# A hybrid encoder layer on one core: value and gate projections moved among output blocks, first tokens transposed on TensorE, x prepared in first slots

## The chip, the cores and the metric

The kernel runs on one core of a Trainium2 chip. The metric is the device time of one execution in microseconds (us). The engines are named as in the profile: PE (TensorE, matrix products), DVE (VectorE), ACT (ScalarE), POOL (GpSimd), and SP, which here only issues DMAs. Each engine runs its own instructions strictly in the order in which the program was written for it.

## The reference

One layer over two sequences (1024 and 4096 tokens, model width 1024), with the same weights:

```python
proj = rms_norm(x, norm_g) @ w_in      # q 512 | k 128 | v 128 | gate 512 | GLU 2 x 512 | gate 512
attn = windowed_gqa(q, k, v, sink)     # 8 heads of 64, 2 kv heads, |t-s| <= 128, 128-query blocks
conv = conformer_conv(u_conv, ...)     # value * sigmoid(gate) -> depthwise conv of 31 taps
                                       # -> LayerNorm -> swish
mix  = concat([attn * silu(g_attn), conv * silu(g_conv)])
y    = rms_norm(x + mix @ w_out, final_g)
```

## The kernel before

The tokens are cut into ten groups of 512 (two from the first sequence, eight from the second), each of four blocks of 128. To keep float32 accuracy with float16 products, every operand is split into a high and a low float16 part, and a product is three matmuls. `inproj` (L413 to L420) thus issues 24 matmuls of 512 columns for one tile of 128 output channels: 8 slices of the model width times 3.

There are two stages. **Stage A** (attention) works with ten weight tiles per group (k, v, four q, four gates). The walk over groups is a walk over "slots", one for each query block: `slot` emits the attention of the block, then work that prepares the groups ahead: `prep_x` for group gi+2 (load a block of x, sum of squares on ACT, reciprocal root on POOL, split on ACT and DVE, transposing DMA), and a share of the projections of group gi+1. At the end of a group `split_late` prepares two weight tiles of stage B. After groups 6 and 7 `max_wout` loads w_out in order to find its largest entry, and `scale_wout` turns that into a power of two; for this it sends one row through PE and back (L396, L402), with two PSUM buffers of the tag `s`, which has three and which the attention scores (L564, L565) use too. Attention results are parked in DRAM.

**Stage B** (convolution and output) has twelve weight tiles per group: eight of value and gate, `glu` (two tiles and two evictions for each of four channel blocks j; L717 on ACT, L718 on DVE, into the tile `h`), and four of the convolution's gate, `conv_gate`. `start_b` loads the 2 MB of transposed x of a group. `conv_chunk` runs the 31 taps of the convolution as DVE instructions (L800 to L804), one for each tap and channel block, in the two pairs j = 0, 1 and j = 2, 3. In all groups but the first the last four taps are made by ACT products (L784, L786) that accumulating DMAs issued by POOL add into `pa`, and the first tap instruction of a pair on DVE (L800) reads `pa`. `ln_batch` transposes the result on PE (L815) and makes the LayerNorm statistics on DVE; `ln_act` transposes back (L854). `out_first` and `out_second` make the output projection of a block (48 matmuls at L873, 24 from the attention half `ma` and 24 from the convolution half `mc`), add x by an accumulating DMA, and normalize (a reciprocal root of seven small steps on POOL, L293 to L301, then L925 on DVE).

The order is not the order of emission. The class `Plan` collects all steps with a cost, their reads and writes, and `flush` lists them anew: whichever step can start first by the costs goes next, and on a tie the one that was emitted first. Two rules of it matter below. Buffers of one tag are handed out in the order in which their first use was emitted. And the resulting order of each engine is fixed; what is late on the chip is waited for in place.

The beginning: `load_first` loads four blocks of x (L237), `prep_first` (L463 to L480) makes squares, one reciprocal root for all four blocks, the split and four transposing DMAs; `first_weights` loads, multiplies by norm_g (L315), scales and splits the weight tiles (L322 to L356).

Of the kernel before, what the change touches and what calls it, by code (L numbers as in the profile page):

```python
# [9 lines left out]
F16 = mybir.dt.float16  # L10
# [7 lines left out]
P = 128  # L18
# [190 lines left out]
def hymba_kernel(ctx, tc, x_p, x_s, w_in, norm_g, sink, dw_w, vecs, w_out, final_g, dist, y_p, y_s):  # L209
# [97 lines left out]
    def load_w(c, early):  # L307
# [5 lines left out]
        dma(lambda: w.t, lambda: w_in[c], 524288, [x16[0]] if 6 <= c < NT_A else [], [w])  # L313
# [146 lines left out]

    def prep_first(x16, xbs):
        ms, v, rs = (small(smx, NB, t, 1) for t in ("ms4", "v4", "rs4"))
        xts = []  # L463
        for b, xb in enumerate(xbs):
            xt = pl.buf(pxA, [P, 2, D], F16, "xt", 2) if b < 2 else pl.buf(pat, [P, 2, D], F16, "pT", 3)
            pl.op("ACT", c_act(1024) + 100, lambda b=b, xb=xb, xt=xt: S.activation(xt.t[:, 1], xb.t, AF.Square, scale=1.0 / math.sqrt(D), accum_out=ms.t[:, b : b + 1]), [xb], [(xt, 1), (ms, b)])
            xts.append(xt)
        pl.op("DVE", 85, lambda: V.tensor_scalar(v.t, ms.t, EPS, XSCALE ** -2, ALU.add, ALU.mult), [ms], [v])
        y = small(smx, NB, "y4", 2, I32)
        pl.op("DVE", 85, lambda y=y: V.tensor_scalar(y.t, v.t.bitcast(I32), -0.5, 1597463007.0, ALU.mult, ALU.add), [v], [y])  # L470
        yv = lambda y=y: y.t.bitcast(F32)
        for it in range(3):
            a, z = small(smx, NB, "a4", 2), rs if it == 2 else small(smx, NB, "z4", 2)
            pl.op("DVE", 105, lambda a=a, yv=yv: V.tensor_tensor(a.t, yv(), yv(), ALU.mult), [y], [a])
            pl.op("DVE", 105, lambda a=a: V.scalar_tensor_tensor(a.t, a.t, -0.5, v.t, ALU.mult, ALU.mult), [a, v], [a])
            pl.op("DVE", 105, lambda a=a, z=z, yv=yv: V.scalar_tensor_tensor(z.t, a.t, 1.5, yv(), ALU.add, ALU.mult), [a, y], [z])
            y, yv = z, (lambda z=z: z.t)
        for b in range(NB):
            split_x(x16, b, xbs[b], xts[b], rs, lambda b=b: rs.t[:, b : b + 1])
        store_x(0, x16)  # L480

# [529 lines left out]
```

## Time and profile before

| | us |
|---|---|
| median of 3 runs (lowest to highest) | 1930.12 (1929.18 to 1932.13) |
| the profiled execution | 1927.47 |
| its span, first to last instruction | 1925.7 |

The profiled execution is 2.65 us under the median, and 1.77 us of it lie around the span. The page gives busy time for each engine, a strip of 40 slices, a chain of work that ended last, and groups of instructions. A busy PE in it is not a PE at its peak. Every view used here names the source line, the engine and the tiles, written `out<-in`; a bracket at the end of a row says how long the engine stood idle before the instruction and what ended the wait. PEclk is the share of the full TensorE clock that was granted.

### The profile page before, as it was taken

The page shows a single profiled execution, that of the slowest core. Times are in us where ns is not written, and L with a number is a line of the kernel's source. Part 1 is how long each engine was busy: PE and PEld are TensorE (multiplying, and loading weights), DVE is VectorE, ACT ScalarE, POOL GpSimd, SP SyncE. Part 2 cuts the span into 40 slices and gives each one's busy share as a digit, 9 for nine tenths or more (in the row PEclk, how much of TensorE's full clock was granted, in tenths as well). Part 3 has the DMA queues.
Part 4 walks back from the last instruction along what each step waited for, and adds up shares of the span by engine and source line. Part 5 has one row for each costly group of instructions (what it writes and reads, how often), then busy time and mean ns, then how long its engine had stood idle before and what let it go on. Part 6 is the DMA issues. An engine that isn't in the chain of part 4 may idle for free.

```text
span 1925.7 us, 25978 instructions
## 1 busy us (share of the span) xinstructions
PE 1816.8 (94%) x8956; PEld 852.0 (44%) x8956; DVE 1666.9 (87%) x3550; ACT 1027.2 (53%) x2181; POOL 606.3 (31%) x830
## 2 busy tenths in 40 slices
PE   3999999999999998989999999999999999999957
PEld 1444444444444443434444444444444444444433
DVE  6688996989999959879989999896969879696997
ACT  3587786887887838754324343433424243434323
POOL 1422233232321200000171725254361717152444
PEclk9999999999999998999999999999999999999979
DMA  8477987999889997664424444443443343443314
GB/s 256 124 156 195 199 198 192 181 234 224 179 211 242 196 267 159 137 169 118 103 69 95 94 88 106 87 110 88 105 103 99 99 105 93 92 117 77 76 56 115
DMA packets 373765, 270.15 MB, mean 140 GB/s; under 512 B 329344, under 2 KB 331008, under 8 KB 371072
## 3 DMA queue, kind: packets, MB, share of 16 engines
q1 hardware_dynamic: 359616, 221.03, 44.6%
q0 software_dynamic: 14016, 47.45, 14.0%
q8 instruction: 70, 1.15, 0.2%
q14 instruction: 63, 0.52, 0.1%
HBM read 100.41 MB, written 58.72 MB: 83 GB/s over the span
## 4 chain that ended last, share of the span: by engine, by line
PE 60%; DVE 24%; ACT 7%; POOL 5%; issue 3%; DMA 1%; SPq 0%; DVEq 0%; ACTq 0%; POOLq 0%
PE mm L420 39%; PE mm L873 15%; DVE acc L804 7%; DVE pe L568 4%; DVE pe L588 3%; ACT pe L576 2%; PE o L603 2%; ACT pe L587 2%; POOL rn_a L300 1%; DVE qst L530 1%; PE s L564 1%; POOL v L916 1%; PE s L565 1%; PE c L854 1%; DVE xt L448 1%
## 5 line engine op out<-in xcount | busy, mean ns | idle before, releaser
L420 PE MATMUL mm<-x,wA 128*128 128x512 f16 x4800 | 1083.3, 381 | 16.8 <-DMA x<-xd 8.8
L420 PEld LDWEIGHTS <-wA 128*128 128x128 f16 x4800 | 468.6, 98 | 562.0 <-issue 23.1
L804 DVE SCALAR_TENSOR_TENSOR acc<-h,taps,acc 128x512 f32<-128x512 f32 (+2 forms) x1244 | 710.1, 640 | 0.0
L873 PE MATMUL mm<-wo,mc 128*128 128x512 f16 x960 | 217.2, 383 | 3.7 <-ACT mc L864 3.5
L873 PE MATMUL mm<-wo,ma 128*128 128x512 f16 x960 | 213.7, 379 | 0.0
L568 DVE CUSTOM_DVE_ANT_0 pe<-s,dist_sb,sink_sb 128x384 f32<-128x384 f32 (+1 forms) x320 | 199.9, 659 | 11.3 <-PE s L565 9.1
L588 DVE SCALAR_TENSOR_TENSOR pe<-pe,rc 128x384 f16<-128x384 f32 (+1 forms) x320 | 189.0, 630 | 15.9 <-ACT pe L587 15.0
L587 ACT ACTIVATE pe<-pe,rc 128x384 f16<-128x384 f32 (+1 forms) x320 | 175.6, 594 | 36.3 <-DVE rc L582 21.3
L576 ACT ACTIVATE pe<-pe,nm 128x384 f32<-128x384 f32 (+1 forms) x320 | 188.5, 590 | 2.4 <-DVE nm L568 2.1
L240 POOL DMA_DIRECT2D pa<-pp x54 | 49.0, 908 | 316.2 <-ACT pp L786 195.7
L873 PEld LDWEIGHTS <-mc 128*128 128x128 f16 x960 | 94.5, 99 | 113.8 <-ACT mc L864 4.1
L873 PEld LDWEIGHTS <-ma 128*128 128x128 f16 x960 | 93.8, 98 | 112.5
L717 ACT ACTIVATE h<-mm,ucolh 128x512 f32<-128x512 f32 x40 | 27.5, 687 | 181.2 <-PE mm L420 181.2
L861 ACT ACTIVATE xn<-c,vec_sb 128x128 f32<-128x128 f32 x160 | 60.2, 457 | 109.7 <-PE c L854 109.7
L564 PE MATMUL s<-kst,qst 128*128 128x384 f16 (+1 forms) x320 | 102.3, 321 | 14.1 <-DVE nm L568 12.0
L420 PE MATMUL mm<-x,xt 128*128 128x512 f16 x480 | 105.6, 379 | 0.0
L300 POOL TENSOR_SCALAR rn_a<-rn_y,v 128x1 f32<-128x1 f32 x76 | 101.6, 1337 | 7.6
L565 PE MATMUL s<-kst,qst 128*128 128x384 f16 (+1 forms) x320 | 101.9, 320 | 0.0
L914 ACT ACTIVATE sq<-yb 128x512 bf16<-128x512 f32 x80 | 49.3, 618 | 97.5 <-DMA yb<-x_s 64.0
L916 POOL TENSOR_SCALAR v<-ms 128x1 f32<-128x1 f32 x38 | 66.1, 1739 | 92.9 <-ACT sq L914 91.1
L440 POOL TENSOR_SCALAR msv<-ms 128x1 f32<-128x1 f32 x36 | 8.5, 236 | 266.6 <-ACT xt L439 266.2
L603 PE MATMUL o<-pT,vst 128*64 128x512 f16 x696 | 84.4, 388 | 0.0
(181 smaller groups left out, 1969.7 us busy)
## 6 DMA issues: line engine op xcount, KB each, us to landing
pa<-pp POOLq DMA_DIRECT2D x48, 512.0 KB, 4.5
xd<-x SPq DMA_DIRECT2D x10, 2048.0 KB, 7.4
x<-xd SPq DMA_DIRECT2D x10, 2048.0 KB, 7.9
xb<-x_s SPq DMA_DIRECT2D x32, 512.0 KB, 4.7
yb<-x_s POOLq DMA_DIRECT2D x30, 512.0 KB, 5.5
y_s<-yb SPq DMA_DIRECT2D x30, 512.0 KB, 2.6
md<-mx SPq DMA_DIRECT2D x40, 256.0 KB, 2.6
ma<-md SPq DMA_DIRECT2D x40, 256.0 KB, 3.1
```

The lines of the kernel that those rows point to most:

```text
L300: pl.op(eng, cost, lambda: en.tensor_scalar(a.t, view(cur), view(cur), v.t, ALU.mult, ALU.mult), [cur, v], [a])
L420: T.matmul(ps.t, w16.t[:, a, k, :], x16.t[:, b, k, :], start=(k == 0 and i == 0), stop=(k == KD - 1 and i == 2))
L564: T.matmul(sv(), q, kst.t[:, 2 * kv, kc0 : kc0 + n], start=True, stop=False)
L565: T.matmul(sv(), q, kst.t[:, 2 * kv + 1, kc0 : kc0 + n], start=False, stop=True)
L568: pl.op("DVE", 198 + n / 0.96, lambda: V.tensor_tensor_reduce(sc_(hh), sv(), dist_b.t[:, kv, d0 : d0 + n], gcol[:, hh : hh + 1], sink_sb[: ...
L576: pl.op("ACT", 280 + 0.834 * n, lambda hh=hh: S.activation(sc_(hh), sc_(hh), AF.Exp, bias=nm.t[:, hh : hh + 1], scale=-1.0, accum_out=den. ...
L587: pl.op("ACT", c_act(n, 1), lambda hh=hh: S.activation(p16(hh, 0), sc_(hh), AF.Copy, scale=rc.t[:, hh : hh + 1]), [rc, (pe, hh + 2)], [(pe ...
L588: pl.op("DVE", c_dve(n, 1), lambda hh=hh: V.scalar_tensor_tensor(p16(hh, 1), sc_(hh), rc.t[:, hh : hh + 1], p16(hh, 0), ALU.mult, ALU.subt ...
L603: T.matmul(o.t[r], vst.t[:, vb % NB, lo, kv, :], mov, start=(i == 0 and m == 0), stop=(i == nk - 1 and m == 2))
L804: pl.op("DVE", c_dve(n, 1), lambda: V.scalar_tensor_tensor(a.t[:, :n], src(), w, a.t[:, :n], ALU.mult, ALU.add), hr + [a], [a])
L873: T.matmul(po[hf].t, m.t[:, a, k - k0, :], wo.t[:, k, b, hf * 512 : (hf + 1) * 512], start=(k == 0 and a == 0 and b == 0), stop=(k == KD - ...
L916: pl.op(eng, 900 if en is GP else 140, lambda: en.tensor_scalar(v.t, ms.t[:, 0:1], ms.t[:, 1:2], EPS, ALU.add, ALU.add), [ms], [v])
```

## The change

Seven edits, all in what is emitted and when:

1. The four first blocks of x are no longer split on ACT and DVE and transposed by DMA. Blocks are scaled in place (DVE for two, ACT for two), PE transposes them in float32 (8 steps of 4 transposes), ACT evicts the high part and DVE the low part. The reciprocal root is made twice, for two blocks each.
2. The first loads come in the order norm_g, x block 0, weight k, x blocks 1 to 3.
3. Group 0 is projected in the order k, v, two gates, four q, two gates, and the weights are made ready in that order.
4. The multiplication by norm_g moves for tiles 3, 5, 6 and 7 to ACT, in eight instructions of 128 columns each.
5. All four `prep_x` of a group are emitted in its first slot.
6. `split_late` is emitted after slots 1 and 2 instead of after the last slot.
7. In stage B `start_b` and `glu` of group gi+2 are emitted among the output blocks of group gi (the load with the first block, the four channel blocks after the second and third), and no longer at the head of group gi+1.

```diff
-        dma(lambda: w.t, lambda: w_in[c], 524288, [x16[0]] if 6 <= c < NT_A else [], [w])
+        dma(lambda: w.t, lambda: w_in[c], 524288, [x16[0]] if 8 <= c < NT_A else [], [w])
+        if c in (3, 5, 6, 7):
+            def by_k():
+                for k in range(KD):
+                    S.activation(w.t[:, k], w.t[:, k], AF.Copy, scale=ng.t[:, k : k + 1])
+            pl.op("ACT", 2340, by_k, [ng, w], [w])
+            return w
...
+    def first_block(x16, b, xb, rs, c):
+        if b % 2 == 0:
+            pl.op("DVE", c_dve2(1024, 1), lambda: V.tensor_scalar(xb.t, xb.t, rs.t[:, c : c + 1], None, ALU.mult), [xb, rs], [xb])
+        else:
+            pl.op("ACT", c_act(1024, 1), lambda: S.activation(xb.t, xb.t, AF.Copy, scale=rs.t[:, c : c + 1]), [xb, rs], [xb])
+        for hf in range(2):
...
+                def tr():
+                    for k in range(4):
+                        T.transpose(pv()[:, k, :], xb.t[:, (4 * hf + k) * P : (4 * hf + k + 1) * P], ident)
+                pl.op("PE", 900, tr, [xb], [pt])
+                pl.op("ACT", c_act(512), lambda: S.activation(dst(0), pv(), AF.Copy), [pt], [(x16, (b, hf, 0))])
+                pl.op("DVE", c_dve(512), lambda: V.tensor_tensor(dst(1), pv(), dst(0), ALU.subtract), [pt, (x16, (b, hf, 0))], [(x16, (b, hf, 1))])
...
-    for t in range(NT_A):
+    for i, t in enumerate((T_K, T_V, 6, 7, 2, 3, 4, 5, 8, 9)):
...
-            for b in range(i * NB // nb, (i + 1) * NB // nb):
+            for b in range(NB if i == 0 else 0):
                 prep_x(gi + 2, x16[gi + 2], b)
...
-        if gi < 6:
-            for c in (2 * gi, 2 * gi + 1):
+            if gi < 6 and i in (1, 2):
+                c = 2 * gi + i - 1
                 wd[c] = split_late(NT_A + c)
...
+    curs[1] = start_b(1, curs[0])
+    load_out(curs[1]["x"])
+    for j in range(4):
+        glu(curs[1], j)
     for gi in range(NG):
         si, g, n_g = groups[gi]
-        if gi + 1 < NG:
-            curs[gi + 1] = start_b(gi + 1, curs[gi])
...
-            for j in range(4):
-                glu(curs[gi + 1], j)
...
                 out_second(gi, b0 + i, po, mc[i], fast(b0 + i, 2))
+                if gi + 2 < NG and nb > 1:
+                    if i == 0:
+                        curs[gi + 2] = start_b(gi + 2, curs[gi + 1])
+                    else:
+                        for j in range(4)[-4 + 2 * (i - 1) :][: 2 if i < nb - 1 else 4]:
+                            if j not in curs[gi + 2].setdefault("glu", []):
+                                curs[gi + 2]["glu"].append(j)
+                                glu(curs[gi + 2], j)
```

What the lists of instructions show of it, at three places. First PE at the very beginning, before the change (`x_0` is the transposed x of group 0, `wA_40` the weight tile k, `w_mx` and `w_mr` largest entries of weights on their way to a power of two):

```order
L330 MATMUL s_213<-ident,w_mx_208 1x128
L341 MATMUL s_226<-w_e_37_218,ones 128x2
L330 MATMUL s_233<-ident,w_mx_224 1x128
L341 MATMUL s_250<-w_e_46_242,ones 128x2
L330 MATMUL s_287<-ident,w_mr_282 1x128
L341 MATMUL s_300<-w_e_70_290,ones 128x2
L420 LDWEIGHTS wA_40_238
L420 MATMUL mm_306<-x_0_259,wA_40_238 128x512
```

and with it:

```order
L337 MATMUL s_201<-ident,w_mx_197 1x128
L348 MATMUL s_230<-w_e_44_224,ones 128x2
L509 MATMUL mm_248<-ident,xb_167 128x128 x4
L509 MATMUL mm_253<-ident,xb_167 128x128 x4
...
L509 MATMUL mm_304<-ident,kst_175 128x128 x4
L509 MATMUL mm_311<-ident,kst_175 128x128 x4
L337 MATMUL s_323<-ident,w_mx_316 1x128
L427 LDWEIGHTS wA_47_286
L427 MATMUL mm_343<-x_0_258,wA_47_286 128x512
```

PE now makes the transposes of x itself (eight rows of four, two of them left out here), and the row that belongs to the scale of the four q tiles (`w_mr`) is no longer ahead of the first projection matmul.

Second, PE in the last stretch of stage A, where the row of `scale_wout` passes (`w_mr` again). Before, with the projections of group 8 around it (`wA_77` and `wA_79` are the third and fourth q tile) and the first scores of group 8 behind it (`kst_6844` is its k):

```order
L420 MATMUL mm_7892<-x_3368_7271,wA_77_339 128x512
L396 MATMUL s_7924<-ident,w_mr_7922 1x128
L420 LDWEIGHTS wA_79_350
L420 MATMUL mm_7926<-x_3368_7271,wA_79_350 128x512
...
L420 MATMUL mm_7926<-x_3368_7271,wA_79_350 128x512
L402 MATMUL s_7944<-w_e_3805_7938,ones 128x2
L564 LDWEIGHTS qst_6294
L564 MATMUL s_7946<-kst_6844,qst_6294 128x384
```

and with the change, where `wA_56` is the tile v of group 8 and `kst_6926` its k:

```order
L427 MATMUL mm_7850<-x_3375_7163,wA_56_389 128x512
L403 MATMUL s_7858<-ident,w_mr_7844 1x128
L427 LDWEIGHTS wA_56_389
L427 MATMUL mm_7850<-x_3375_7163,wA_56_389 128x512
...
L409 MATMUL s_7909<-w_e_3812_7871,ones 128x2
L598 LDWEIGHTS qst_6421
L598 MATMUL s_7911<-kst_6926,qst_6421 128x384
L599 LDWEIGHTS qst_6421
L599 MATMUL s_7911<-kst_6926,qst_6421 128x384
```

The row goes through PE in the second projection tile of group 8, no longer in the sixth, and the scores of group 8 follow there. Before, no score stands on PE between the last ones of group 7 and this row, which is 153 projection matmuls; with the change the longest such stretch anywhere in stage A is 96.

Third, DVE where the last group (9) begins in stage B. Before (`h_8325` is the tile h of group 9, the rows L819 are the statistics of group 8, `pa_16824` the ACT products of group 9, `acc_8778` its sum):

```order
L718 SCALAR_TENSOR_TENSOR h_8325_15998<-h_8325_15998,mm_16787 128x512
L925 SCALAR_TENSOR_TENSOR yb_16715<-yb_16715,r_8309_16885,fg 128x1024
L718 SCALAR_TENSOR_TENSOR h_8325_15998<-h_8325_15998,mm_16881 128x512
L819 BN_STATS bst_17013<-c_17002 128x6
L718 SCALAR_TENSOR_TENSOR h_8325_15998<-h_8325_15998,mm_16941 128x512
...
L837 SCALAR_TENSOR_TENSOR nmr_17065<-mv_17030,lrs_17064 128x4
L800 SCALAR_TENSOR_TENSOR acc_8778_17089<-h_8325_15998,taps,pa_16824 128x512
L800 SCALAR_TENSOR_TENSOR acc_8778_17096<-h_8325_15998,taps,pa_16824 128x512
L804 SCALAR_TENSOR_TENSOR acc_8778_17089<-h_8325_15998,taps,acc_8778_17089 128x512
```

and with it, under the new line numbers (L755 evicts a value tile into h, L837 is the first tap of a pair, L841 a tap, L856 the statistics; `h_8194`, `acc_8785` and `pa_16731` are those of group 9):

```order
L902 TENSOR_TENSOR mc_16860<-xn_16842,mc_16860 128x512
L755 SCALAR_TENSOR_TENSOR h_8194_15949<-h_8194_15949,mm_16873 128x512
L837 SCALAR_TENSOR_TENSOR acc_8785_16974<-h_8194_15949,taps,pa_16731 128x512
L837 SCALAR_TENSOR_TENSOR acc_8785_16984<-h_8194_15949,taps,pa_16731 128x512
L841 SCALAR_TENSOR_TENSOR acc_8785_16974<-h_8194_15949,taps,acc_8785_16974 128x512
...
L962 SCALAR_TENSOR_TENSOR yb_16878<-yb_16878,r_8315_17023,fg 128x1024
L755 SCALAR_TENSOR_TENSOR h_8194_15949<-h_8194_15949,mm_16932 128x512
L841 SCALAR_TENSOR_TENSOR acc_8785_16974<-h_8194_15949,taps,acc_8785_16974 128x512
...
L856 BN_STATS bst_17119<-c_17094 128x6
```

With the change the first tap of group 9 stands behind the eviction of its third channel block, and 23 tap instructions of group 9 stand ahead of the statistics of group 8; before, none does. The eviction of the fourth channel block (the second L755 row) stands behind the tap that reads `pa`.

## Rows read from the trace of the kernel before

**Rows 1.** Windows: length; busy PE, PEld, DVE, ACT, POOL; PEclk; DMA share; GB/s.

```profile
104.00:860.00 756.00, 726.38 (x3806) 337.61 (x3804) 654.33 (x1656) 585.89 (x1357) 157.23 (x355) 0.99 0.86 195
1100.00:1765.00 665.00, 665.00 (x3173) 312.92 (x3172) 566.86 (x925) 247.18 (x467) 274.46 (x259) 1.00 0.41 98
1765.00:1926.00 161.00, 128.41 (x604) 62.34 (x602) 145.67 (x336) 55.86 (x119) 63.85 (x66) 0.91 0.33 81
```

**Rows 2.** Timeline, opening: start, length, engine, line, operation.

```profile
4.08 1.06 ACT L466 ACTIVATE xt<-xb 128x1024 f16<-128x1024 f32 x1 [2.05 <-DMA xb<-x_p]
9.29 1.06 ACT L466 ACTIVATE pT<-kst 128x1024 f16<-128x1024 f32 x1
10.96 1.22 DVE L315 TENSOR_TENSOR pe<-pe,ng 128x1024 f32<-128x1024 f32 x1
26.32 5.31 SPq L243 DMA_TRANSPOSE x<-pT  x2
34.17 0.35 SPq L237 DMA_DIRECT2D xd<-x  x1
36.45 17.84 PE L420 MATMUL mm<-x,wA 128*128 128x512 f16 x69
```

**Rows 3.** Timeline, other stretches: prices of the operations that are added.

```profile
57.22 0.66 PE L517 MATMUL s<-ident,vt 128*128 128x128 f32 x4
58.76 0.67 DVE L522 TENSOR_TENSOR vst<-s,vst 128x512 f16<-128x512 f32 x1
...
731.07 2.12 ACT L587 ACTIVATE pe<-pe,rc 128x384 f16<-128x384 f32 x4
...
1770.37 0.16 DVE L829 TENSOR_SCALAR lv<-mv 128x4 f32<-128x4 f32 x1
...
1772.54 0.16 DVE L837 SCALAR_TENSOR_TENSOR nmr<-mv,lrs 128x4 f32<-128x4 f32 x1
```

**Rows 4.** Waits of PE from 104 to 860: total us, times, longest.

```profile
PE s L564 <- DVE nm L568: 11.8, 19, 1.5
PE mm L420 <- DVE qst L530: 6.8, 1, 6.8
PE s L341 <- DVE w_e L337: 3.5, 3, 2.0
```

**Rows 5.** Timeline of DVE and ACT, 700 to 720.

```profile
704.46 1.22 DVE L389 TENSOR_REDUCE wmx<-xb 128x1 f32<-128x1024 f32 x1 [7.60 <-DMA xb<-w_out]
...
718.23 0.63 ACT L610 ACTIVATE mx<-t 128x512 f16<-128x512 f32 x1 [20.90 <-DVE t L609]
```

**Rows 6.** Timeline of PE, then of DVE, 1750 to the end.

```profile
1724.19 41.60 PE L420 MATMUL mm<-x,wA 128*128 128x512 f16 x192
1765.63 1.91 PE L815 MATMUL c<-ident,acc 128*128 128x128 f32 x16
...
1853.92 0.48 PE L815 MATMUL c<-ident,wA 128*128 128x128 f32 x1 [11.90 <-DVE wA L804]
...
1756.19 0.69 DVE L718 SCALAR_TENSOR_TENSOR h<-h,mm 128x512 f32<-128x512 f32 x1 [7.71 <-ACT h L717]
1766.27 0.70 DVE L819 BATCH_NORM_STATS2 bst<-c 128x6 f32<-128x512 f32 x1 [9.39 <-PE c L815]
...
1772.62 1.41 DVE L800 SCALAR_TENSOR_TENSOR acc<-h,taps,pa 128x512 f32<-128x512 f32 x2
...
1779.79 16.64 DVE L804 SCALAR_TENSOR_TENSOR acc<-h,taps,acc 128x512 f32<-128x512 f32 x25
...
1902.03 0.70 DVE L819 BATCH_NORM_STATS2 bst<-c 128x6 f32<-128x512 f32 x1 [1.60 <-PE c L815]
```

**Rows 7.** Timeline of DVE and POOL around 958, then POOL around 1760.

```profile
955.89 15.98 DVE L804 SCALAR_TENSOR_TENSOR acc<-h,taps,acc 128x512 f32<-128x512 f32 x24
...
958.94 13.11 POOL L916 TENSOR_SCALAR v<-ms 128x1 f32<-128x1 f32 x1 [0.24 <-ACT sq L914]
...
1759.55 0.86 POOL L240 DMA_DIRECT2D pa<-pp  x1 [4.20 <-DMA pa<-pp]
```

More of the change, by code (lines that the diff above doesn't have):

```diff
@@ L459, in load_first @@
         return xb
-    def prep_first(x16, xbs):
[L462 to L479, printed above, removed]
-        store_x(0, x16)
@@ new lines, in square_first, with chain @@
+    def square_first(xbs):
+        ms = [small(smx, 2, "ms4", 2) for _ in range(NB // 2)]
+        for b, xb in enumerate(xbs):
+            sq = pl.buf(pxA, [P, 2, D], F16, "xt", 2)
+            m = ms[b // 2]
+            pl.op("ACT", c_act(1024) + 190, lambda b=b, xb=xb, sq=sq, m=m: S.activation(sq.t[:, 1], xb.t, AF.Square, scale=1.0 / math.sqrt(D), accum_out=m.t[:, b % 2 : b % 2 + 1]), [xb], [sq, (m, b % 2)])
+        return ms
+    def prep_first(x16, xbs):
+        for i, ms in enumerate(square_first(xbs)):
+            v, a, rs = (small(smx, 2, t, 2) for t in ("v4", "a4", "rs4"))
+            y = small(smx, 2, "y4", 2, I32)
+            def chain(ms=ms, v=v, a=a, rs=rs, y=y):
+                V.tensor_scalar(v.t, ms.t, EPS, XSCALE ** -2, ALU.add, ALU.mult)
+                V.tensor_scalar(y.t, v.t.bitcast(I32), -0.5, 1597463007.0, ALU.mult, ALU.add)
+                z = y.t.bitcast(F32)
+                for it in range(3):
+                    V.tensor_tensor(a.t, z, z, ALU.mult)
+                    V.scalar_tensor_tensor(a.t, a.t, -0.5, v.t, ALU.mult, ALU.mult)
+                    V.scalar_tensor_tensor(rs.t, a.t, 1.5, z, ALU.add, ALU.mult)
+                    z = rs.t
+            pl.op("DVE", 1900, chain, [ms], [v, a, rs, y])
+            for b in (2 * i, 2 * i + 1):
+                first_block(x16, b, xbs[b], rs, b % 2)
+        store_x(0, x16)
@@ L616, in hymba_kernel @@
     smA = pool(st_a, "smA", side="right")
-    wA, wd = [], {}
+    wA, wd = {}, {}
     x16 = {0: new_x16(0)}
     own = {0: new_group(0)}
-    xbs = [load_first(b) for b in range(NB)]
     dma(lambda: ng.t, lambda: norm_g, 4096, [], [ng])
+    xbs = [load_first(0)]
     w_k = load_w(T_K, True)
+    xbs += [load_first(b) for b in range(1, NB)]
     prep_first(x16[0], xbs)
@@ L637, in hymba_kernel @@
     dma(lambda: taps, lambda: dw_w, 63488, [], [taps_b])
+    first_weights([T_G])
+    first_weights([T_G + 1])
     first_weights([2, 3, 4, 5])
@@ L647, in hymba_kernel @@
     x16[1] = new_x16(1)
-    for t in range(NT_A):
+    for i, t in enumerate((T_K, T_V, 6, 7, 2, 3, 4, 5, 8, 9)):
         group_proj(0, x16[0], own[0], None, t)
-        if t < 4:
-            first_weights([T_G + t])
-        elif t < 4 + NB:
-            prep_x(1, x16[1], t - 4, [x16[0]])
+        if t in (6, 7):
+            first_weights([t + 2])
+        elif 4 <= i < 4 + NB:
+            prep_x(1, x16[1], i - 4, [x16[0]])
     def slot(gi, blocks, i, qb):
@@ L676, in hymba_kernel @@
             slot(gi, blocks, i, qb)
-        if gi < 6:
-            for c in (2 * gi, 2 * gi + 1):
+            if gi < 6 and i in (1, 2):
+                c = 2 * gi + i - 1
                 wd[c] = split_late(NT_A + c)
-        else:
+        if gi >= 6:
             if gi == 6:
```

11 lines of the change are left out of this document (6 added, 5 removed).

## The prediction

> **What bounds the kernel now.** I read the stages first, each as one window [rows 1]. From 1100 to 1765 us PE is busy for 665.00 us of 665.00 at full granted clock, DVE for 567: there PE alone sets the time, and nothing that moves work on other engines can shorten it. Before that, from 104 to 860 us (stage A), PE is busy for 726 of 756 us, with DVE at 654 and the DMA engines at 0.86: PE paces it too, but it loses 30 us in waits. After it, from 1765 to the end, PE is busy for 128 of 161 us and DVE for 146: the end belongs to DVE. And ahead of all, the first projection matmul runs at 36.45 us [rows 2]. So there are three places to win: the opening, the waits in stage A, the end. The timeline shows what each hangs on. In the opening the fourth block of x is squared at 9.29, the last pair of transposing DMAs goes at 26.32 and takes SP 5.31 us, the store of the finished x, which needs the last of them, goes at 34.17, and PE starts 2.3 us later [rows 2]. In stage A the largest waits of PE are for scores (11.8 us in 19 pieces), one of 6.8 us, and 3.5 us for the scale of a weight [rows 4]. The 6.8 us have a history: ACT stood idle for 20.90 us up to 718 and DVE for 7.60 us up to 704, where it waits for a block of w_out [rows 5]. `scale_wout` holds two of the three `s` buffers in the queue of that tag, so that no score of group 8 can be placed ahead of it, and PE runs projections only; then the scores come in a heap, and PE waits for the softmax. At the end, finally, PE does the LayerNorm transposes of group 8 at 1765.63; DVE, which had idled 7.71 and 9.39 us just before, starts the taps of group 9 at 1772.62 and is busy to the end; PE has nothing left at 1842.0 and waits 11.90 us for these taps [rows 6].
>
> **The opening.** Removed: the split on DVE (four instructions of about 1.2 us) and four transposing DMAs. Added, with prices from [rows 3]: 8 x 4 transposes on PE at 0.66 us for four (5.3 us, at a time when PE has nothing else), 8 evictions on ACT and 8 on DVE (0.67), a second root of 11 steps (twelve take 2.33 us, so 2.1), and 32 ACT instructions of 128 columns. For the last, ACT takes 1.06 us for 1024 columns [rows 2] and 0.53 for 384 (a quarter of 2.12 [rows 3]), which makes 0.32 for 128 and 0.64 for 512. The path, by the new order of each engine: weight k now lands between x blocks 0 and 1. Five loads came within 6.9 us after the first (4.08 to 10.96 [rows 2]), some 1.7 us each, so that the second block lands at 8.5 and the fourth at 11. First root: square of block 1 at 9.8, eleven steps, 12.1. Second root behind four scalar steps (0.8) and one scaling (0.8): 15.7. From there ACT has in a row: scaling of block 3 (1.06), three evictions (1.9), the split of k (1.06), one eviction (0.64), eight small instructions (2.5), three evictions (1.9): 24.8, and DVE's last subtraction 25.5. First projection matmul at 25.5 in place of 36.45, **11 us** sooner. Two of them are lost again: v can't start before its weight has gone through DVE (0.8 of scalar steps, two maxima of about 1.2, another 1.2 of scalar steps, one product of 1.2, one split of 1.3 after 25.5, so 32.4; PE is done with k at 31.7), and the scales of later tiles stand within the k and v matmuls. **-9 us**. Bounds: -4 if the small ACT instructions cost what 384 columns cost (0.2 us more each, with up to 24 of them ahead of the v tile), -12 if nothing is lost.
>
> **Stage A.** The number of matmuls, scores and softmax steps stays. With all `prep_x` in the first slot, the blocks of w_out that `max_wout` loads get their buffers sooner, and the row of `scale_wout` passes PE four projection tiles earlier, with scores around it. The heap goes, and with it the 6.8 us [rows 4]. The two PE steps of a late weight's scale now always have matmuls between them, so most of the 3.5 us goes as well. The 11.8 us for scores I leave. **-9 us**. Bounds: what is late next is the softmax, since the first slot now carries four preparations on ACT and DVE beside attention; if the waits for scores grew by half I would lose 6, with the rest unchanged a net of +3. If half of the 30 us of PE's waits went, -15. I take the value near the row that has a cause.
>
> **Stage B up to 1765.** The load of x for group gi+2 is issued a whole iteration sooner, and two channel blocks are projected between output blocks. PE was full and stays full: 0. Between 860 and 1100 the same DVE work and the same first load open the stage: 0, bounds -4 and +4.
>
> **The end.** 23 taps of group 9 now stand ahead of the statistics of group 8. One costs 16.64/25 = 0.67 us [rows 6], so 15.3 us of the DVE work that PE waited for moves into the 7.71 + 9.39 = 17.1 us in which DVE idled. The last LayerNorm transposes but for those of the single closing block come at 1853.92 - 15.3 = 1838.6. PE must not be later than that: it was through at 1842.0, but 22 matmuls of an output block, 0.217 us each (192 take 41.60 [rows 6]), now follow the transposes in place of preceding them, 4.8 us, so 1837.2. From there DVE has the same 48 us up to the closing statistics at 1902.03 [rows 6] as before, and the tail behind it stays. **-15 us**; bounds -8 (if `pa` or the normalization on POOL holds DVE back half as long as it idled) and -18.
>
> **Sum.** -9 - 9 - 15 = -33 on the profiled execution of 1927.47, which is 1894.5. The median of the runs shown lies 2.65 above that execution, so I forecast **1897 us**.
>
> **Rivals.** *The opening's gain dies in stage A.* If stage A were paced by DMA or softmax and not by PE, an earlier start would only lengthen the waits; speaking for it are DMA shares of 0.86 and DVE at 87%, against it 96% on PE [rows 1]. Only the end is left: 1930 - 15 = 1915. *The end doesn't move*, because DVE waits in place for `pa` where it idled before: 1930 - 18 = 1912. For it speaks that POOL adds three times in series, the last add issued at 1759.55 [rows 7], some 6 us ahead of the transposes of group 8; against it, that the second channel block now ends four tiles and two output blocks ahead of these transposes (192 matmuls at 0.217 us, 42 us), and before four tiles (21 us). *The order hardly changes the chip's time*, as each piece was hidden already: 1930.
>
> *Slower.* The eviction of the fourth channel block stands on DVE behind the tap that reads `pa`. If `pa` is late, that PSUM buffer stays full and PE stops, in each of the eight groups from 2 to 9. The price is lateness beyond a point: two tiles and an output block (96 matmuls, 21 us) lie between the third block and the transposes, the buffer is needed 7 us behind these (the transposes, 1.9 us, and one tile, 5.2 us), 7 us of DVE work stand between, so `pa` may come 21 us after the third block. I expect it 3 us before that block: some 18 us after the second one, as before (tiles done at 1724.19 + 20.8 [rows 6], last add issued at 1759.55 [rows 7], and its transfer). Lateness of 24 us costs nothing; to lose the 33 us won and 7 on top takes 5 us per group more, so 29 us, and gives 1937. The trace shows a cause that could do it: a POOL step on one value per partition took 13.11 us at 958.94, and ended just when the row of 24 taps on DVE ended (955.89 + 15.98 = 971.87) [rows 7]. Two to three such steps in every group ahead of the adds would be enough. The Trainium skill (GPSIMD Engine Reference, section 1, Specifications) says that POOL shares its SBUF interfaces with VectorE and contends with DVE instructions that have two SBUF inputs. By that rule the taps that now fill DVE's pauses slow POOL's steps more often than before; this trace agrees with it at 958.94, by the 13.11 us beside the 16 us of taps. It makes me leave the end's bound at -8. Against the rival: POOL was busy for 274 us of 665 in stage B [rows 1], stretched steps included.
>
> **How the numbers follow.** Forecast with its terms in their bounds (1882 to 1910): 0.64. Opening lost in stage A: 0.14. End not moved: 0.13. No change: 0.03. Slower: 0.06. About 0.2% (4 us) is what a measurement of this kernel tells from no change. Faster 0.64 + 0.14 + 0.13 = 0.91, same 0.03, slower 0.06. The range takes the forecast's own 1882 and reaches up to the two rivals at 1912 and 1915, so 1882 to 1916; outside are the rivals of no gain, and the tails of the bounds.
>
> **What would show it.** First projection matmul at 24 to 28 us. In stage A no wait of PE for a score's PSUM or for q above 3 us near the end, and its idle time under 24 us. From 1100 on PE at 100% as before. DVE without a pause in the 20 us ahead of the transposes of group 8, and the wait of PE ahead of those of group 9 (11.90 us) down to under 3. The prediction is wrong if stage A ends less than 10 us sooner than before, or if PE shows gaps in the middle of stage B behind an eviction of value tiles.

## Result and profile after

The changed kernel takes 1900.03 us (median of 4 runs, 1897.10 to 1902.05) against 1929.65 for the kernel before on the same chip: a ratio of 0.9847, 95% interval 0.9833 to 0.9860, so 29.6 us faster. The profiled execution took 1898.89 us, with a span of 1897.1 (before 1927.47 and 1925.7).

I follow the lead from mark to mark. First the windows of the changed kernel (length; busy PE, PEld, DVE, ACT, POOL; PEclk; DMA share; GB/s), beside [rows 1]:

```profile
0.00:104.00 104.00, 85.94 (x398) 42.34 (x398) 76.29 (x178) 67.76 (x130) 27.41 (x75) 0.97 0.64 181
104.00:838.00 734.00, 715.85 (x3762) 332.85 (x3758) 650.74 (x1647) 580.00 (x1344) 155.73 (x355) 1.00 0.86 198
1100.00:1250.00 150.00, 143.85 (x676) 67.26 (x674) 143.97 (x256) 56.82 (x108) 66.13 (x54) 0.98 0.42 104
1250.00:1750.00 500.00, 499.26 (x2381) 234.88 (x2380) 431.52 (x689) 184.56 (x353) 210.52 (x199) 1.00 0.41 97
1750.00:1898.00 148.00, 128.09 (x601) 60.61 (x599) 131.26 (x313) 54.65 (x120) 66.02 (x74) 0.93 0.36 91
```

The first 104 us of the kernel before, which the earlier rows don't have:

```profile
0.00:104.00 104.00, 70.14 (x320) 32.89 (x321) 68.56 (x152) 50.74 (x82) 28.68 (x77) 1.00 0.62 185
```

**Opening.** At 104 us PE has been busy for 15.8 us more than before. Of these, 7.6 us are the new transposes (3.67 + 1.08 + 2.82 in the timeline), so the rest of PE's work is 8.2 us ahead. The timeline of the opening, beside [rows 2]:

```profile
4.87 1.06 ACT L473 ACTIVATE xt<-xb 128x1024 f16<-128x1024 f32 x1 [2.85 <-DMA xb<-x_p]
...
10.52 1.06 ACT L473 ACTIVATE xt<-kst 128x1024 f16<-128x1024 f32 x1
...
18.72 2.44 ACT L317 ACTIVATE pe<-pe,ng 128x128 f32<-128x128 f32 x8
...
22.18 0.38 PE L427 MATMUL mm<-x,wA 128*128 128x512 f16 x1
```

The fourth block of x is squared at 10.52, and the first projection matmul starts at 22.18, 14.3 us sooner. Eight small ACT instructions take 2.44 us.

**Stage A.** PE is idle for 734 - 715.85 = 18.2 us, before 29.6. PE's waits from 104 to 838 (total us, times, longest), beside [rows 4]:

```profile
PE s L337 <- DVE w_mx L329: 8.2, 6, 2.7
PE s L598 <- DVE nm L602: 4.2, 6, 1.2
PE s L551 <- ACT vt L546: 2.8, 3, 1.5
PE s L598 <- DVE vst L556: 1.2, 1, 1.2
```

The 6.8 us wait is gone and the waits for the softmax (`nm`) fell from 11.8 to 4.2; a new kind costs 8.2, the wait for the largest entry of a late weight tile (`w_mx`). The first matmul of stage B proper (the x of group 1) comes 19.5 us sooner. First before, then after:

```profile
865.18 5.06 PE L420 MATMUL mm<-x,wA 128*128 128x512 f16 x16 [8.85 <-DMA x<-xd]
```

```profile
845.71 54.45 PE L427 MATMUL mm<-x,wA 128*128 128x512 f16 x240 [8.29 <-DMA x<-xd]
```

Up to these two rows PE idles from 104 us on for 25.9 us (741.71 - 715.85), before for 34.8 (761.18 - 726.38; 3.7 of the 29.6 above were the beginning of the wait for this x). So of the 19.5 us the opening has 8.2, less idling 8.9, and the remaining 2.4 is busy time of the same matmuls. Part of these 2.4 may lie behind the 6.8 us wait, where the kernel before had a granted clock of 0.74; how much is not shown:

```profile
720.00:740.00 20.00, 11.54 (x49) 5.05 (x48) 17.82 (x51) 19.11 (x49) 0.00 (x0) 0.74 0.67 141
```

**Stage B.** From there to the LayerNorm transposes of group 8 it is 900.4 us before (1765.63) and 904.3 after (1750.05), 3.9 us given back. First before, then after, up to 1100 us:

```profile
865.18:1100.00 234.82, 226.82 (x1058) 106.24 (x1059) 226.28 (x474) 87.57 (x158) 82.10 (x74) 0.98 0.40 98
```

```profile
845.71:1100.00 254.29, 251.50 (x1179) 116.72 (x1180) 227.91 (x470) 93.68 (x164) 76.33 (x71) 0.99 0.39 93
```

The 3.9 us are a net. Up to 1100 us PE idles 2.8 us, before 8.0; from there on it idles 6.9, before nothing; and the same matmuls take 2.2 us more busy time. PE is full again from 1250 on, but not from 1100 to 1250. The place, PE at the transposes of group 2, then DVE in the midst of the statistics:

```profile
1130.99 1.47 PE L852 MATMUL c<-ident,acc 128*128 128x128 f32 x12
1132.30 7.93 PE L910 MATMUL mm<-wo,ma 128*128 128x512 f16 x36
1142.28 0.66 PE L891 MATMUL c<-ident,xn 128*128 128x128 f32 x4 [2.05 <-ACT xn L882]
1145.20 1.11 PE L891 MATMUL c<-ident,xn 128*128 128x128 f32 x4 [2.26 <-ACT xn L882]
1146.65 7.55 PE L910 MATMUL mm<-wo,mc 128*128 128x512 f16 x24 [0.33 <-ACT mc L901]
```

```profile
1135.05 1.29 DVE L962 SCALAR_TENSOR_TENSOR yb<-yb,r,fg 128x1024 f32<-128x1024 f32 x1 [1.68 <-POOL r L301]
```

36 matmuls cover the statistics of group 2. On DVE an output normalization stands between these statistics, and waits 1.68 us for its reciprocal root from POOL. PE then waits for the first normalized block (2.05 us) and, with no matmul left between the two, for the second (2.26 us); the 24 matmuls behind take 7.55 us in place of the 5.34 that 24 take elsewhere.

**The end.** PE, then DVE, beside [rows 6]:

```profile
1750.05 1.91 PE L852 MATMUL c<-ident,acc 128*128 128x128 f32 x16
...
1821.85 0.33 PE L852 MATMUL c<-ident,wA 128*128 128x128 f32 x1 [0.15 <-DVE wA L841]
...
1823.98 4.91 PE L910 MATMUL mm<-wo,ma 128*128 128x512 f16 x22
1830.33 0.65 PE L891 MATMUL c<-ident,xn 128*128 128x128 f32 x4 [1.43 <-ACT xn L882]
...
1834.92 8.15 PE L910 MATMUL mm<-wo,mc 128*128 128x512 f16 x24 [1.02 <-ACT mc L901]
...
1871.85 0.60 PE L852 MATMUL c<-ident,acc 128*128 128x128 f32 x4
```

```profile
1730.25 0.69 DVE L755 SCALAR_TENSOR_TENSOR h<-h,mm 128x512 f32<-128x512 f32 x1 [12.64 <-ACT h L754]
...
1741.22 8.69 DVE L841 SCALAR_TENSOR_TENSOR acc<-h,taps,acc 128x512 f32<-128x512 f32 x13
1750.69 1.30 DVE L856 BATCH_NORM_STATS2 bst<-c 128x6 f32<-128x512 f32 x2 [0.78 <-PE c L852]
...
1872.48 0.70 DVE L856 BATCH_NORM_STATS2 bst<-c 128x6 f32<-128x512 f32 x1 [1.48 <-PE c L852]
```

DVE goes from taps into the statistics with a pause of 0.78 us (before 9.39); its long pause, 12.64 us, now lies ahead of the eviction of the third channel block. And PE's 11.90 us wait is gone. Between the transposes of groups 8 and 9 lie 71.8 us, before 88.3. Behind them it is 75.3 us to the end of the span, before 71.8.

The account of the spans, in us: opening -8.2, stage A -11.3, stage B +3.9, groups 8 to 9 -16.5, tail +3.5: -28.6.

### The profile page after: what moved, and what is told of

Read it like the earlier page. It is cut to its first block, busy times and chain, and to the rows that moved or that the text cites. A ratio compares the mean times of both kernels' runs of the same rounds, so it can differ in the third digit from the quotient of the medians.

```text
span 1897.1 us, 26070 instructions
## 1 busy us (share of the span) xinstructions
PE 1824.5 (96%) x8988; PEld 854.7 (45%) x8988; DVE 1669.4 (88%) x3565; ACT 1038.3 (55%) x2219; POOL 602.1 (32%) x828
## 4 chain that ended last, share of the span: by engine, by line
PE 56%; DVE 20%; ACT 9%; POOL 6%; issue 5%; DMA 4%; SPq 0%; DVEq 0%; ACTq 0%; POOLq 0%
PE mm L427 35%; PE mm L910 16%; DVE pe L602 4%; DVE acc L841 3%; ACT pe L610 2%; DVE pe L622 2%; POOL rn_a L300 2%; PE o L637 2%; ACT pe L621 2%; DVE qst L564 2%; POOL v L953 2%; PE s L598 1%; PE s L599 1%; POOL rn_y L301 1%; DMA yb<-x_p 1%
## 5 line engine op out<-in xcount | busy, mean ns | idle before, releaser
L841 DVE SCALAR_TENSOR_TENSOR acc<-h,taps,acc 128x512 f32<-128x512 f32 (+2 forms) x1244 | 711.7, 642 | 0.0
L622 DVE SCALAR_TENSOR_TENSOR pe<-pe,rc 128x384 f16<-128x384 f32 (+1 forms) x320 | 185.0, 617 | 22.9 <-ACT pe L621 21.5
L953 POOL TENSOR_SCALAR v<-ms 128x1 f32<-128x1 f32 x38 | 76.1, 2002 | 145.6 <-ACT sq L951 144.7
L943 ACT ACTIVATE yb<-mm,inv 128x512 f32<-128x512 f32 x76 | 47.9, 681 | 74.4 <-PE mm L910 74.3
```

What stands on the lines that cost most here:

```text
L622: pl.op("DVE", c_dve(n, 1), lambda hh=hh: V.scalar_tensor_tensor(p16(hh, 1), sc_(hh), rc.t[:, hh : hh + 1], p16(hh, 0), ALU.mult, ALU.subt ...
L841: pl.op("DVE", c_dve(n, 1), lambda: V.scalar_tensor_tensor(a.t[:, :n], src(), w, a.t[:, :n], ALU.mult, ALU.add), hr + [a], [a])
L953: pl.op(eng, 900 if en is GP else 140, lambda: en.tensor_scalar(v.t, ms.t[:, 0:1], ms.t[:, 1:2], EPS, ALU.add, ALU.add), [ms], [v])
```

## Experiments

All times are medians; the difference is to the kernel before, run beside it. O stands for edits 1 to 4 (opening), P for 5 (all `prep_x` in the first slot), L for 6 (late weight tiles among the slots), G for 7 (`start_b` and `glu` among the output blocks).

| kernel | edits | us | ratio to before (95%) | difference, us |
|---|---|---|---|---|
| e1 | O | 1931.15 | 1.0015 (1.0006 to 1.0024) | +2.4 |
| e3 | P | 1928.96 | 0.9999 (0.9990 to 1.0008) | +0.2 |
| e4 | L | 1970.87 | 1.0217 (1.0203 to 1.0231) | +42.1 |
| e2 | G | 1919.37 | 0.9951 (0.9939 to 0.9964) | -9.4 |
| e5 | O L G | 1957.73 | 1.0145 (1.0128 to 1.0162) | +28.1 |
| e6 | O P G | 1910.02 | 0.9896 (0.9880 to 0.9912) | -19.6 |
| e7 | P L G | 1914.38 | 0.9922 (0.9908 to 0.9936) | -15.3 |
| e8 | O P L | 1908.50 | 0.9890 (0.9874 to 0.9906) | -21.1 |
| changed | O P L G | 1900.03 | 0.9847 (0.9833 to 0.9860) | -29.6 |

### One edit alone: e1 to e4

e1 is the changed kernel with these three pieces as before:

```diff
-            for b in range(NB if i == 0 else 0):
+            for b in range(i * NB // nb, (i + 1) * NB // nb):
...
-            if gi < 6 and i in (1, 2):
-                c = 2 * gi + i - 1
-                wd[c] = split_late(NT_A + c)
+        if gi < 6:
+            for c in (2 * gi, 2 * gi + 1):
+                wd[c] = split_late(NT_A + c)
...
-    curs[1] = start_b(1, curs[0])
-    load_out(curs[1]["x"])
-    for j in range(4):
-        glu(curs[1], j)
```

(with the rest of edit 7). e2, e3 and e4 are the kernel before with edit 7, 5 or 6 of the change alone.

> The kernel before with edits 1 to 4 alone (the opening). Forecast theory: first projection matmul some 13 us sooner, as the profile of the changed kernel has it, about 4 of them lost again in the first 100 us, the rest kept to the end: -9 us, ratio 0.995, and stage B's first matmul about 9 us sooner than 865.18. Rival (the gain dies in stage A, which DMA or softmax would pace): first matmul as early, stage B's start and the time within 3 us of the kernel before, ratio 0.999 to 1.001.

> The kernel before with edit 7 alone (projections of stage B among the output blocks). Forecast theory, its term for the end: -15 us, ratio 0.992. Second theory, from the profile of the changed kernel: 17 us gained between the LayerNorm transposes of groups 8 and 9, some 5 given back behind them and some 4 lost between 1130 and 1150 us where PE waits for the normalized block: -9 us, ratio 0.995, with these PE waits there again. Rival (the end doesn't move): within 3 us, ratio 0.999 to 1.001.

> The kernel before with edit 5 alone (all prep_x of a group in its first slot). Forecast theory: this edit alone lets the row of scale_wout pass among scores; the 6.8 us wait near 720 goes, -7 us, ratio 0.9965, stage B's first matmul near 858. Rival: four preparations in one slot crowd the softmax, waits of PE for scores (11.8 us before) grow by half, net 0 to +3 us, ratio 1.000 to 1.0015.

> The kernel before with edit 6 alone (two weight tiles of stage B prepared behind the second and third slot). Forecast theory: the waits of PE for the scale of a weight (3.5 us) go for the most part, -3 us, ratio 0.9985; the 6.8 us wait stays. Rival, from the profile of the changed kernel, in which PE waits 8.2 us in six pieces for the largest entries of a weight: this edit makes those waits, +5 us, ratio 1.0025. Third possibility: those waits belong to edit 5, and the time stays within 2 us.

**e1: the rival's time holds, its reason only in part.** The first projection matmul comes at 22.45 and stage B at 868.01, 2.8 us later than before. Stage A and one of the places where the lead goes:

```profile
104.00:860.00 756.00, 719.18 (x3776) 334.18 (x3773) 644.50 (x1641) 580.86 (x1345) 160.97 (x355) 0.99 0.84 193
```

```profile
536.97 0.38 PE L348 MATMUL s<-w_e,ones 1*128 1x2 f32 x2 [2.71 <-DVE w_e L344]
```

Without the beginning of the wait for x at the window's end, PE idles 35.3 us there, in the kernel before 25.9. The waits for the softmax did not grow (10.8 us, before 11.8 [rows 4]). What grew are the waits for x from a transposing DMA (3.9 us, before 1.2) and, most, the two kinds for the scale of a weight (6.4 and 3.9 us, before 3.5):

```profile
PE s L348 <- DVE w_e L344: 6.4, 5, 2.7
```

The time at which each group's finished x is stored shows the lead in passing (issue of the `xd` store, us):

| x of group | 0 | 1 | 2 | 3 | 4 | 5 | 6 | 7 | 8 | 9 |
|---|---|---|---|---|---|---|---|---|---|---|
| before | 34.2 | 92.2 | 150.4 | 238.1 | 313.8 | 389.3 | 465.4 | 534.8 | 616.0 | 684.1 |
| e1 (O) | 24.0 | 86.7 | 146.9 | 237.0 | 304.8 | 381.2 | 457.5 | 542.2 | 612.0 | 689.9 |
| e4 (L) | 33.5 | 91.7 | 162.0 | 261.6 | 328.8 | 419.7 | 503.0 | 586.1 | 643.9 | 728.8 |
| changed | 23.7 | 85.2 | 132.2 | 209.7 | 274.5 | 362.2 | 429.8 | 504.1 | 577.1 | 657.1 |

In e1 the lead shrinks from 10.2 to 1.1 us by group 3, is back at 8 to 9, and turns into a lag of 7.4 between the stores of groups 6 and 7, 84.7 us apart in place of 69.4, where PE waits among others for the scale of a late weight tile (the row at 536.97). At group 8 x is 4.0 us ahead once more, at group 9 5.8 behind.

**e2: the second theory holds.** -9.4 us, by the profile in its parts too: PE waits 2.06 us for the first normalized block of group 2, and the transposes of groups 8 and 9 (1770.14 and 1841.93) lie 72 us apart, as in the changed kernel.

**e3: no gain.** The 6.8 us wait for q did go, as the forecast theory says, but the waits for the softmax grew by 7 us, as its rival says, and a wait for k came (30 to 868 us):

```profile
PE s L564 <- DVE nm L568: 18.9, 22, 3.4
...
PE mm L420 <- DVE kst L508: 4.8, 1, 4.8
```

Two causes I had as alternatives, both true, sum to nothing.

**e4: 42 us slower**, eight times the rival's 5 and of its sign. Waits for a weight's largest entry are the smaller part (8.7 us); PE waits mostly for the softmax (104 to 870 us):

```profile
PE s L564 <- DVE nm L568: 32.7, 18, 5.5
```

and x is stored 12 us late for group 2, 24 for group 3 and 45 for group 9 (table).

### One edit undone: e5 to e8

Each is the changed kernel with the lines of one edit as before. e5 has the first pair of lines of the diff above, e6 the second piece. e7 has this piece, and `prep_first`, the order of group 0 and the multiplication by norm_g as before:

```diff
+    xbs = [load_first(b) for b in range(NB)]
     dma(lambda: ng.t, lambda: norm_g, 4096, [], [ng])
-    xbs = [load_first(0)]
     w_k = load_w(T_K, True)
-    xbs += [load_first(b) for b in range(1, NB)]
```

e8 has edit 7's loops as before:

```diff
+        if gi + 1 < NG:
+            curs[gi + 1] = start_b(gi + 1, curs[gi])
...
+            for j in range(4):
+                glu(curs[gi + 1], j)
```

> The changed kernel with edit 5 undone (x of a group prepared over its four slots again, the late weight tiles still behind slots 2 and 3). Theory of the shared buffers (a weight tile and a block of x take the same two load buffers and two split buffers, in the order of emission, so that a tile emitted between blocks delays the group's last block; alone it cost 42 us): some 40 us slower than the changed kernel, 1940, ratio to the kernel before 1.005. Rival (what edit 6 costs alone comes from an order of PE that is unlucky by chance): within 10 us of the changed kernel, ratio 0.985 to 0.990.

> The changed kernel with edit 6 undone (both late weight tiles behind the last slot again). Theory A: with the blocks of x ahead of them the early place of the tiles neither costs nor pays; the time is that of the changed kernel within 4 us, ratio to the kernel before 0.983 to 0.987, and the 8.2 us of PE's waits for a weight's largest entry shrink. Theory B: edits 5 and 6 pay only as a pair (alone they gave 0 and +42 us), so without edit 6 the opening's gain dies in stage A again: 1915 to 1920, ratio 0.993 to 0.996.

> The changed kernel with edits 1 to 4 undone (the opening as before). Theory A (stage A is freed by edits 5 and 6, and an earlier opening then shows whole): 13 us slower than the changed kernel, 1913, ratio to the kernel before 0.992. Theory B (the opening's gain never reaches the end; edits 5 and 6 give all of stage A's share): same as the changed kernel within 4 us, ratio 0.983 to 0.987. Theory C (edits 5 and 6 give nothing; only the three together do): 1919, ratio 0.995.

> The changed kernel with edit 7 undone (projections of stage B at the head of a group again). Theory A (the part from stage B on is independent of the rest, and edit 7 is worth the 9.5 us that it gave alone): 1909, ratio to the kernel before 0.990; stage B's first matmul at 846 as with the whole change. Rival (edit 7 is needed to carry an earlier stage B to the end): 1918 or more, ratio 0.995 or more.

**e5**: 57.7 us over the changed kernel; the theory of the shared buffers has the sign, the size was 40. **e6**: 10 us over the changed kernel, between A and B: PE's `nm` waits are 16.9 us (with edit 6 they are 4.2) and one for k is 5.4, while those for a weight's largest entry are gone. So edit 6 takes away 18 us of waits and adds 8.2 of its own. **e7**: theory A, 1914.38 where 1913 was expected; here the opening is worth 14.3 us, where alone it cost 2.4. **e8**: edit 7 is worth 8.5 us on top of the others, 9.4 alone: it is the one edit whose worth hardly depends on the others. Yet stage B starts at 849.59 in e8, 3.9 us later than in the changed kernel, where theory A had the same 846. Its profile has stage B full in the middle (from 849.59 to the transposes of group 8 at 1749.84, 900.3 us) and the old wait at the end:

```profile
1837.66 0.48 PE L852 MATMUL c<-ident,wA 128*128 128x128 f32 x1 [11.42 <-DVE wA L841]
```

### Where the late tiles stand: e9, e10

A late tile takes one of two load buffers (tag `xb`) and one of two split buffers (tag `xt`), as each block of x does.

```diff
             for b in range(NB if i == 0 else 0):
                 prep_x(gi + 2, x16[gi + 2], b)
+                if gi < 6 and b in (1, 2):
+                    wd[2 * gi + b - 1] = split_late(NT_A + 2 * gi + b - 1)
```

e10 has, behind that loop:

```diff
+            if gi < 6 and i == 0:
+                for c in (2 * gi, 2 * gi + 1):
+                    wd[c] = split_late(NT_A + c)
```

> The changed kernel with the two late weight tiles emitted in the first slot, one behind the second and one behind the third block of x, in place of behind slots 2 and 3. All four blocks of x stay in the first slot. Theory of the shared buffers (it is the tiles' place in the row of load and split buffers that holds the last blocks of x back): like e5, at least 20 us slower than the changed kernel, 1920 to 1955, and x of groups 2 and 3 stored later than the 132 and 210 us of the changed kernel. Rival (what costs is that x is spread over the slots, wherever the tiles stand): within 5 us of the changed kernel, ratio to the kernel before 0.983 to 0.988.

> The changed kernel with both late weight tiles emitted in the first slot, right behind the four blocks of x. Theory of the shared buffers: x of the group is not delayed, the tiles are done earlier, time within 4 us of the changed kernel, ratio to the kernel before 0.983 to 0.987. Rival (the two PE steps of a tile's scale, for which PE waits 8.2 us in the changed kernel, come still earlier among the scores): PE's waits for a weight's largest entry grow to 12 us or more and the time by 4 or more, ratio 0.987 to 0.990.

e9 takes 1972.66 us, ratio 1.0221 (1.0189 to 1.0252), 72.6 us over the changed kernel; I had the sign, and 1955 as its upper end. The blocks of x stay in the first slot, only the tiles stand between them, and PE now waits for x itself, 26.4 of the 65.6 us that it idles from 104 to 835:

```profile
PE mm L427 <- DMA x<-xt: 26.4, 6, 5.8
```

SP shows it for the x of group 2, in e9 and then in the changed kernel:

```profile
121.37 0.43 SPq L237 DMA_DIRECT2D xb<-w_in  x1
...
129.96 1.21 SPq L237 DMA_DIRECT2D xb<-x_s  x1
...
159.90 0.54 SPq L237 DMA_DIRECT2D xd<-x  x1
```

```profile
106.09 0.58 SPq L237 DMA_DIRECT2D xb<-x_s  x1
...
117.86 0.53 SPq L237 DMA_DIRECT2D xb<-w_in  x1
...
132.18 0.53 SPq L237 DMA_DIRECT2D xd<-x  x1
```

The row `xb<-x_s` is the load of the group's fourth block: in e9 at 129.96, behind both weight tiles, in the changed kernel at 106.09, ahead of both. So the place of the tiles among the blocks of x is what costs; that is shown. How much of it the shared buffers make is not: the steps of a tile now also stand ahead of those of a block in the order of ACT and POOL. ACT waits 2.71 us for a tile's scale at 116.53, and squares the third block, whose load was issued at 108.87, only at 118.68.

e10 takes 1915.09, ratio 0.9923 (0.9897 to 0.9948), 15 us over the changed kernel, and both theories are wrong about why: x of groups 2 and 3 is stored earlier still (125.6 and 195.9), waits for a weight's largest entry fall to 3.1 us, but from 250 to 400 PE idles for 22.6 us:

```profile
PE s L598 <- DVE nm L602: 17.5, 7, 6.2
```

The result of the fifth query block is stored at 239.7 there, in the changed kernel at 212.6: attention is put back. It is the second slot of a group that is late, the one behind the slot with four blocks and two tiles: in group 0 its result is stored at 169.0 in place of 145.1, and the fifth block is the second slot of group 1. By what is not settled.

### The gap at group 2, and a planner's number: e11, e12

```diff
-                            if j not in curs[gi + 2].setdefault("glu", []):
+                            if j not in curs[gi + 2].setdefault("glu", []) and not (gi == 1 and j > 1):
                                 curs[gi + 2]["glu"].append(j)
                                 glu(curs[gi + 2], j)
+                if gi == 1 and nb == 1:
+                    glu(curs[3], 2)
+                    glu(curs[3], 3)
```

> The changed kernel with the third and fourth channel block of group 3 emitted behind the single closing block of group 1, no longer behind its third block. The gates of group 3 then follow the LayerNorm transposes of group 2 on PE in place of preceding them, and cover the statistics. Theory (the 4 us that stage B lost near 1140 us are PE's wait for the first normalized block of group 2, with the slower matmuls behind it): 3 to 5 us faster than the changed kernel, 1895 to 1897, ratio to the kernel before 0.982 to 0.9835, PE busy for 149 or more of 150 us from 1100 to 1250. Rival (DVE paces that stretch, with 144 us of 150, and the wait only moves): within 2 us of the changed kernel, ratio 0.984 to 0.986.

e11 takes 1891.36 us (1888.62 to 1892.48), ratio 0.9791 (0.9769 to 0.9814), faster than both kernels. PE at group 2, and the transposes of group 8:

```profile
1123.88 2.75 PE L427 MATMUL mm<-x,xt 128*128 128x512 f16 x12
1126.62 0.66 PE L891 MATMUL c<-ident,xn 128*128 128x128 f32 x4
1127.11 7.93 PE L427 MATMUL mm<-x,xt 128*128 128x512 f16 x36
...
1743.75 1.91 PE L852 MATMUL c<-ident,acc 128*128 128x128 f32 x16
```

DVE there:

```profile
1117.51 1.28 DVE L962 SCALAR_TENSOR_TENSOR yb<-yb,r,fg 128x1024 f32<-128x1024 f32 x1
...
1119.37 1.29 DVE L856 BATCH_NORM_STATS2 bst<-c 128x6 f32<-128x512 f32 x2
```

48 gate matmuls now stand on both sides of the normalized block, and PE does not wait for it; it is busy for 149.51 of 150 us from 1100 to 1250. Ahead of that block there are again 36 matmuls (24 and 12), so their number is not what differs. The order on DVE differs too: the output normalization stands ahead of the statistics, and doesn't wait for POOL. e11 changes both orders at once and does not tell their shares apart. Stage B up to group 8 now takes 897.2 us, 7.1 less than in the changed kernel. I had expected 3 to 5, from the 3.9 us that stage B had lost. But that was a net: the pauses of 4.3 us and the 2.2 us by which the matmuls behind were slower are more than that by themselves.

```diff
-            pl.op("DVE", 1140, lambda w=w, i=i: V.tensor_reduce(mx.t[:, i : i + 1], w.t, AX.XY, ALU.max, apply_absolute_value=True), [w], [(mx, i)])
+            pl.op("DVE", 1140 if early else 3000, lambda w=w, i=i: V.tensor_reduce(mx.t[:, i : i + 1], w.t, AX.XY, ALU.max, apply_absolute_value=True), [w], [(mx, i)])
```

> Kernel e11 with one number more: the planner's cost of the DVE step that finds a late weight tile's largest entry goes from 1140 to 3000 ns, so that the planner lists PE's transpose of that entry later among the matmuls. No instruction is added or removed. Theory (PE's 8.1 us of waits at that transpose come from a fixed order that was laid out with too early a time for the step): these waits fall under 2 us and the time by 4 to 7 us against e11, 1884 to 1888, ratio to the kernel before 0.976 to 0.978. Rival (every shift of the list makes waits of other kinds of the same size): waits at that transpose fall but the time stays within 3 us of e11 or grows, ratio 0.978 to 0.982.

e12 takes 1895.08 us, ratio 0.9834 (0.9817 to 0.9852). The waits at that transpose are gone and stage B starts 4.2 us sooner than in e11 (842.34), so the theory holds in stage A; but the list changed everywhere, and at the first LayerNorm PE waits where it had not:

```profile
915.19 2.71 PE L852 MATMUL c<-ident,acc 128*128 128x128 f32 x10 [3.36 <-DVE acc L841]
```

By the transposes of group 8 (1746.10) the 4.2 us are lost and 2.4 more: the rival holds for the time.

## Why the prediction was right

The range held the time, and 1897 is 3 us from it. The three places to win were the right ones, and each gave what was forecast within 2.3 us; inside the terms, errors that cancel had a part in this, and that is luck. By its own steps:

- **Opening, -9: measured -8.2.** The path was shorter than forecast (22.18, not 25.5: the second root was through at 14.6, not 15.7, and the last of ACT's evictions at 22.6, not 24.8), but of the 14.3 us PE lost 6 behind it, not 2. The wait for the weight of v, for which the 2 stood, did not come. Of the 6, PE idles 4.2 us more between the first projection matmul and 104 us (4.4, before 0.2; the longest waits are 1.88 us for the softmax at 81.92 and 1.45 for x from a transposing DMA at 85.35), and 1.8 are short matmuls for weight scales, which ran ahead of the first projection matmul before and run behind it now. Too long a path and too small a loss cancel.
- **Stage A, -9: measured -11.3, by other terms.** The 6.8 us went, as forecast. The waits for scores, which I left at 11.8, fell to 4.2. The 3.5 us for scales became 8.2 us for largest entries, where I had "most of it goes". That these two deviations nearly cancel, 7.6 us less than forecast and some 7 more, is luck. The step that failed is the division: I priced the opening and stage A as terms that add, each with a cause of its own. Alone, the opening gave +2.4 us, edit 5 +0.2, edit 6 +42.1; together with each other -21.1 (e8). My rival that the opening's gain dies in stage A, which I gave 0.14, is what edits 1 to 4 do by themselves, though not by waits for the softmax, as it had it, but mostly by those for weight scales (e1); edit 5 and then edit 6 keep it from happening. That edit 6 is a danger without edit 5 I had not seen at all: I had treated "x prepared earlier" and "weights prepared earlier" as independent, and they share four buffers and the order of ACT and POOL.
- **Stage B, 0: measured +3.9.** "PE was full and stays full" failed at one place, group 2, whose gates moved ahead of its LayerNorm. The order of the new kernel shows that; I had looked at the boundary of groups 8 and 9 alone. It left no matmul between the first two normalized blocks, hence the second wait (2.26 us). The first (2.05 us) is no lack of matmuls: 36 cover the statistics here and in e11, 33 in group 8, where PE does not wait. It is mostly DVE's 1.68 us of waiting for POOL in the midst of the statistics; without that some 0.4 us would be left (an estimate, 2.05 - 1.68; read from the trace, no run changes it alone). "0" between 860 and 1100 failed the other way, by 5.2 us less idling.
- **The end, -15: measured -13.0.** 16.5 us gained ahead of the transposes of group 9 for 15.3 forecast (23 taps), and 3.5 lost behind. The step that failed is "the same 48 us up to the closing statistics": it became 50.6 (1821.85 to 1872.48; before 48.1), as an output normalization (1.28 us) and three taps of the single closing block (0.97) moved from ahead of these transposes to behind them on DVE. The 22 matmuls behind them on PE came as forecast. The rest, 0.9 us, is behind the closing statistics, where the last 24 matmuls take 7.12 us, before 5.74.
- **Slower, by a late `pa`:** not seen; in stage B no eviction of a value tile holds PE. But its cause was at work. DVE waits for a reciprocal root of POOL 12.8 us in all from 1100 to 1750, before 6.2, and POOL's steps were stretched as before, one of them beside 18 taps:

```profile
1121.53 10.79 POOL L953 TENSOR_SCALAR v<-ms 128x1 f32<-128x1 f32 x1 [2.44 <-ACT sq L951]
```

  The Trainium skill (GPSIMD Engine Reference, section 1, Specifications) names the contention of POOL with DVE instructions that have two SBUF inputs; this trace agrees, by the 10.79 us for a step that takes 0.28 at its shortest. The step ended at 1132.32, when the 18 taps and the two first taps behind them were done (1132.16). It belongs to the root for which DVE then waits the 1.68 us at group 2, so it had a part in what stage B lost.

Of the signs named, these came true: stage A's idle time under 24 us (18.2), no wait for a score's PSUM or q near its end, the 11.90 us wait under 3 (two of 0.15 and 0.33). DVE without a pause in the 20 us ahead of the transposes of group 8 came true in the main: it idles 2.1 of them, before 16.5, but its pause of 12.64 us ends just as they begin. First matmul at 24 to 28 (22.18) and PE at 100% from 1100 on did not. Neither sign of being wrong came: stage A ended 19.5 us sooner, and the gaps in stage B are behind normalized blocks and taps, not behind evictions.

## What to carry to other kernels

Where a planner lays out one fixed order, edits need not add: measure each alone and each undone before giving it a share of the gain, and look first at what they share (here four load and split buffers, and the fixed order of the engines). When work is moved away from a place, count what covers the latency that stays there, and look at what stands in that latency on the other engines; a few tiles put back at group 2 were worth 7 us. And a planner's better number for one step can still lose, since it moves every other step too.

## What the runs showed of the hardware

Pauses of PE cost more than their length here. In the changed kernel two waits of 2.05 and 2.26 us, with four transposes between them, were followed by 24 matmuls in 7.55 us; in e11, without the waits, the same kind took 5.34. The granted clock from 1136 to 1154 was 0.81 of full, a mix of its two levels, 1.2 and 2.4 GHz; PE had been idle for most of 1140 to 1146 before:

```profile
1136.00:1154.00 18.00, 13.36 (x52) 5.81 (x51) 17.62 (x40) 6.28 (x13) 0.00 (x0) 0.81 0.19 59
```

The Trainium skill (TensorE: Matmul & The Clock Gate, Part 1) says that the idle array's clock is gated and that activity releases it; this trace agrees, by 7.55 against 5.34 us.
